# Halved weight places and a seven-block second expert layer in a two-layer diffusion backbone

## The chip, the core and the metric

The program runs on one core of a Trainium2 chip, as one launch. The metric is the device time of that launch in microseconds. The engines that matter here are TensorE (PE in the profile; PEld is its weight load, which overlaps), VectorE (DVE), ScalarE (ACT), GpSimd (POOL) and the sync engine SP, whose queue issues nearly all loads from HBM; ACT's queue issues a few.

## The reference, cut to what matters

Two layers act on 256 latent tokens and 256 context tokens of width 1024. Each layer has a mixer (layer 0: grouped attention beside a Fourier mix; layer 1: differential attention), then a mixture of 16 experts, each a gated MLP of inner width 512. A token takes one group of four experts and, in it, the best two:

```python
g_idx = jnp.argmax(g_logits, axis=-1)
e_sel = jnp.take_along_axis(e_logits, g_idx[:, None, None], axis=1)[:, 0]
top_p, top_i = lax.top_k(jax.nn.softmax(e_sel, axis=-1), TOP_K)
...
def expert_step(acc, params):
    wg, wu, wd, gate = params
    y = (jax.nn.silu(tok @ wg) * (tok @ wu)) @ wd
    return acc + gate[:, None] * y, None
```

Layer 0 runs its experts on 512 tokens (1024 choices), layer 1 on the 256 latent tokens (512 choices). All weights are float32: an expert has three matrices of 2 MB (gate, up, down), so a layer's experts are 96 MB.

## The kernel before

**Slots and blocks.** The experts of a layer are ranked by how many tokens chose them (four of layer 1, two of layer 0 are fixed experts that keep the last ranks, so that their weights can be fetched before the ranking is known). `CAPS` gives each rank a number of slots, `PLAN` packs the slots into blocks of 128 rows. Kind "m" is one expert of 128 slots, "p" two of 64, "q" four of 32, and "w" is made of the two largest: one block of 128 slots for each and one block that holds the ends of both, 64 + 64. Layer 1 has eight blocks: block 0 (ranks 12 to 15), 1 (rank 3), 2 (rank 2), 3 (the ends of ranks 0 and 1), 4 (rank 0), 5 (rank 1), 6 (ranks 8 to 11), 7 (ranks 4 to 7). Should an expert have more tokens than slots, a general path behind a branch computes the rest. With these inputs the counts of layer 1 are 141, 127, 70 and 56 for ranks 0 to 3 and at most 27 behind them, so the branch is not taken before, nor with the slots of the changed kernel.

**Products.** Each block goes through three products: G (gate), U (up) and D (down). G and U are eight steps over the 128-row slices of the weights (`gate_up`), D is four slices for two halves of the output (`down`), again eight steps. In one step every expert of the block has a matmul of its own: its 128, 64 or 32 slots are the columns of the array that it uses, and 512 columns of its weights stream through. So a step has one matmul (128 wide), two (64 wide each, side by side) or four (32 wide). Ahead of a block's G stand 48 small matmuls that pick its tokens (`pick`), between U and D four transposes (`tr`), and behind D eight matmuls that scatter the result to the tokens (`sp`). In layer 1 the order of the 24 products is written out by hand in `TURNS`; the order of single instructions on an engine inside that is set when the program is built.

**Weights.** `piece` gives out places of 16 KB for each of the 128 partitions, 2 MB: a ring of four (`RING`), and further ones in rooms that are free at that time (`more["first"]`, `more["order"]`; in layer 1 nine places in all, 18 MB). One place holds one matrix of an expert, and one DMA fills it (`load`). A place comes free when the last matmul on it is done. `Experts.todo` lists the loads in the order of the products, and `issue` puts the next ones on SP's queue. In layer 0 the last three loads, the up matrix of rank 7 and the down matrices of ranks 6 and 7, stand on ACT's queue behind the output writes (`yd`) of the last block but one, since their places come free late. The same places carry the modulation weights (`wada`) and the projections (`win`, `wi`, `wo`).

Of the kernel before, what the change touches and what calls it, by code (L numbers as in the profile page):

```python
# [19 lines left out]
P = 128  # L20
D = 1024
KT = 8
# [11 lines left out]
    (192, 192) + (128,) * 2 + (32,) * 12,  # L34
)

# [3 lines left out]
    (("q", 12, 13, 14, 15), ("m", 3), ("m", 2), ("w", 0, 1), ("q", 8, 9, 10, 11), ("q", 4, 5, 6, 7)),  # L40
# [28 lines left out]
TURNS = ("G0 U0 G1 U1 D0 D1 G6 G4 U6 U4 G3 G5 D6 U3 D4 U5 D3 D5 G7 G2 U2 U7 D2 D7")  # L69
# [96 lines left out]
def hybrid_kernel(ctx: ExitStack, tc: tile.TileContext, A: dict, dbg=None):  # L166
# [4 lines left out]
    RING = 4  # L171
# [159 lines left out]
    def ada_load(l, pair, q, after=None):  # L331
        w = piece([P, 2, 2048], "wada")
        src = A["w_ada"][l].rearrange("(p k) n -> p k n", p=P)
        load(w, src[:, 2 * q:2 * q + 2, 2048 * pair:2048 * pair + 2048], after)
        ada_w[l, pair, q] = w

    def ada_mm(l, pair, q):
        if q == 0:
            ada_ps[l, pair] = aux("ada")
        ps = ada_ps[l, pair]  # L340
        w = ada_w.pop((l, pair, q))
        for k in range(2):
            kt = 2 * q + k
            for j in range(4):
                T.matmul(ps[32 * j:32 * j + 32], cs[:, kt, :], w[:, k, 512 * j:512 * j + 512],  # L345
                         start=(kt == 0), stop=(kt == KT - 1))
# [29 lines left out]
    def ada_first_load(s):  # L376

        w = piece([P, KT, 2, 256], "wada0")
        src = A["w_ada"][0].rearrange("(p k) (g n) -> p k g n", p=P, g=6)
        nc.sync.dma_start(w, src[:, :, 0:2, 256 * s:256 * s + 256])  # L380
        ada_w["first", s] = w
# [12 lines left out]
    def ada_first(s):  # L394
        w = ada_w.pop(("first", s))
        ps = aux("ada")
        for kt in range(KT):
            for j in range(4):
                T.matmul(ps[32 * j:32 * j + 32, 0:128], cs[:, kt, :], w[:, kt, j // 2, 128 * (j % 2):128 * (j % 2) + 128],
                         start=(kt == 0), stop=(kt == KT - 1))  # L400
# [34 lines left out]
    def load_cols(name, src, c0, n=512, after=None):  # L435
        w = piece([P, KT, n], name)
        load(w, src.rearrange("(k p) n -> p k n", p=P)[:, :, c0:c0 + n], after)
        return w

    def project(wk, hT, groups, tick, order=None, start=None, early=None):  # L440
# [10 lines left out]
        for i in range(-n, len(flat) + AHEAD):  # L451
# [4 lines left out]
            if i < 0 or n <= i < len(flat):  # L456
# [6 lines left out]
                split(*parts[j], w()[:, kt, :])  # L463
# [18 lines left out]
    def out_project(wk, yT, w, g1, tbs, hook, done, place):  # L482


        for h in range(2):
            sp = [[wk.tile([P, 512], F32R, name="wo", bufs=KT), place[:, kt, :]] for kt in range(KT)]
            for n, tb in enumerate(tbs):
                ps = mm()
                for kt in range(KT):
                    if n == 0:  # L490
                        split(*sp[kt], w[h][:, kt, :])
# [12 lines left out]
    def layer_even(fill):  # L504
# [7 lines left out]
        w_a = piece([P, KT, 512], "win")  # L512
        for s in range(4):
# [6 lines left out]
            nc.sync.dma_start(w_a[:, 2 * s:2 * s + 2, :], src[:, 2 * s:2 * s + 2, 512:1024])  # L520
# [468 lines left out]
    class Experts:  # L989


        def __init__(self, l):
# [3 lines left out]
            self.todo = list(dict.fromkeys((r, which) for which, b in products(l) for _, _, r in blocks[b]))  # L996
# [3 lines left out]
        def issue(self, n=None, after=None, queue=None):  # L1000
            n = len(self.todo) if n is None else n
            for r, which in self.todo[:n]:
                self.load(r, which, after, queue)
            del self.todo[:n]

        def load(self, r, which, after, queue):
# [8 lines left out]
            w, src = weights(pick, which, lambda s, n: piece(s, n, True))  # L1015
            load(w, src, after, queue)
            self.w[r, which] = w
# [11 lines left out]
    def weights(pick, which, place):  # L1029
        w = place([P, KT, 512] if which < 2 else [P, 4, D], "we")  # L1030
        return w, pick(A[("w_gate", "w_up", "w_down")[which]]).rearrange("(p k) n -> p k n", p=P)

    def moe(l, ntb, experts, yp, yT, finish, w_o, place, after_loads):
# [8 lines left out]
        if l == 0:  # L1042
            hp = more["H"] = left("h2")
            rows_of = hp.tile([P, ntb, D], F32, name="h2", tag="piece", bufs=1)
        h2 = [xt[:, 2 + tb, :] if l else rows_of[:, tb, :] for tb in tbs]


        if l:
            fp = more["F"] = left("first")
            experts.issue(1)  # L1050
# [131 lines left out]
        experts.issue(2 - l)  # L1182
# [156 lines left out]
        experts.issue(len(fixed) - 2 + l)  # L1339
# [135 lines left out]
        if l == 0:  # L1475
# [10 lines left out]
            experts.issue(1)  # L1486
            experts.issue(len(experts.todo) - 7)
            g2 = piece([P, nv + 2, D], "g2", True)
# [17 lines left out]
        experts.issue(len(experts.todo) - (0 if l else 3))  # L1506
# [117 lines left out]
        def weights_at(i, k):  # L1624
            which, b = ops[i]
            w = experts.w[blocks[b][0][2], which]
            return w[:, k, :] if which < 2 else w[:, k // 2, 512 * (k % 2):512 * (k % 2) + 512]
# [8 lines left out]
        def gate_up(which, bi, amid):  # L1636

            ps = mm("gu")
            for kt in range(KT):
# [7 lines left out]
                for _, n_, r in blocks[bi]:  # L1647
                    T.matmul(ps[c:c + n_], xTs[bi][0][:, kt, c:c + n_], experts.w[r, which][:, kt, :],  # L1648
# [13 lines left out]
        def down(bi, amid, final):  # L1662
# [7 lines left out]
            for f in range(4):  # L1670
# [3 lines left out]
                for h in range(2):  # L1674
# [5 lines left out]
                    for _, n_, r in blocks[bi]:  # L1680
                        T.matmul(ps[h][c:c + n_], aTs[bi][0][:, f, c:c + n_],  # L1681
                                 experts.w[r, 2][:, f, 512 * h:512 * h + 512], start=(f == 0), stop=(f == 3))
# [9 lines left out]
            else:  # L1692
# [8 lines left out]
                if bi == len(blocks) - 2:  # L1701
                    for _ in range(3):
# [3 lines left out]
        for i, (which, bi) in enumerate(ops):  # L1706
# [22 lines left out]
            if final and which == 0:  # L1729
# [3 lines left out]
                after_loads(gather(0, [g2[:, nv + k, :] for k in range(2)]))  # L1733
# [8 lines left out]
        with tc.If(rv > 0):  # L1742
            if l == 0:
                more["first"] = 2 * ["E"] + ["H"]
            spare = lambda s, n: piece(s, n, True)
# [14 lines left out]
            with tc.For_i(0, NE, 1) as e:  # L1760
# [3 lines left out]
                with tc.If(nc.values_load(some[0:1, 0:1], min_val=0, max_val=1) > 0):  # L1764
                    ws = []
                    for i in range(3):
                        w, src = weights(pick, i, spare)
                        G.dma_start(w, src)
                        ws.append(w)
                    rc = un.tile([P, ntb], F32, name="rc")  # L1770
                    G.dma_start(rc, restd[bass.ds(e, 1)].rearrange("o p t -> (o p) t"))
                    for tb in range(ntb):
# [16 lines left out]
                        for which in range(2):  # L1789
                            ps = tr("gu")  # L1790
                            for kt in range(KT):
                                T.matmul(ps, xT_[:, kt, :], ws[which][:, kt, :], start=(kt == 0), stop=(kt == KT - 1))
# [9 lines left out]
                        for h in range(2):  # L1802
                            ps = tr("dn")
                            for f in range(4):
                                T.matmul(ps, aT[:, f, :], ws[2][:, f, 512 * h:512 * h + 512], start=(f == 0), stop=(f == 3))
# [73 lines left out]
    def second_parts(n):  # L1879

        return more["X"].tile([P, KT, 512], F32R, name="lo", tag="piece", bufs=n)

    yp, yT = layer_even(fill0)
    more["first"] = 4 * [None] + ["X"] + 2 * ["E"]
    place = second_parts(1)
    more["order"] = [None, "H"] + 3 * [None] + ["X"] + 2 * ["E"]
    ex = Experts(0)
    ex.issue(4)
# [18 lines left out]
    def first_experts():  # L1907
        more["first"], more["order"] = [], 2 * [None] + 2 * ["X"] + 2 * [None] + ["F", "X", "E"]
        w_odd["place"] = second_parts(3)
        ex = Experts(1)  # L1910
        ex.issue(6)
# [39 lines left out]
```

## Time and profile before

| | before |
|---|---|
| runs | 1064.57, 1067.69, 1064.04 us; median 1064.57 us |
| the profiled execution | 1060.02 us, its span 1058.3 us |
| TensorE busy | 977.3 us, 92% of the span |
| VectorE, ScalarE, GpSimd busy | 53%, 38%, 5% |
| moved by DMA | 309.81 MB, 293 GB/s over the span |
| second expert layer, first product to last | 814.96 to 1043.2 us |

The profiled execution lies 4.55 us below the median of the runs. In the profile a 512-column float32 matmul leaves two records, and four 32-wide matmuls that run side by side leave eight, so counts of instructions ("x64") are records. A row of the timeline joins neighbours of one line and sometimes of several widths; the width named is that of the first.

### The profile page before, as it was taken

The page shows a single profiled execution, that of the slowest core. Times are in us where ns is not written, and L with a number is a line of the kernel's source. Part 1 is how long each engine was busy: PE and PEld are TensorE (multiplying, and loading weights), DVE is VectorE, ACT ScalarE, POOL GpSimd, SP SyncE. Part 2 cuts the span into 40 slices and gives each one's busy share as a digit, 9 for nine tenths or more (in the row PEclk, how much of TensorE's full clock was granted, in tenths as well). Part 3 has the DMA queues.
Part 4 walks back from the last instruction along what each step waited for, and adds up shares of the span by engine and source line. Part 5 has one row for each costly group of instructions (what it writes and reads, how often), then busy time and mean ns, then how long its engine had stood idle before and what let it go on. Part 6 is the DMA issues. An engine that isn't in the chain of part 4 may idle for free. (4 is left out here: it accounts for less than half of the span.)

```text
span 1058.3 us, 14182 instructions
## 1 busy us (share of the span) xinstructions
PE 977.3 (92%) x5205; PEld 573.3 (54%) x5205; DVE 556.4 (53%) x1354; ACT 397.3 (38%) x817; POOL 48.9 (5%) x73
## 2 busy tenths in 40 slices
PE   3899999897999899999978999998788999999995
PEld 3676555686455454666423578875565444434531
DVE  3565465877456543677327557438787223214324
ACT  4255343643235233666205435327764211100111
POOL 3000100100100000000021000000000000000000
PEclk9999999999999999999988999999998999999998
DMA  9969877535779998999897674433155999969891
GB/s 287 367 272 384 341 324 280 212 128 217 299 289 429 387 430 354 358 357 351 314 367 275 232 256 159 145 121 133 50 210 195 399 427 427 427 272 426 360 408 41
DMA packets 52546, 309.81 MB, mean 293 GB/s; under 512 B 4432, under 2 KB 12832, under 8 KB 35064
## 3 DMA queue, kind: packets, MB, share of 16 engines
q1 hardware_dynamic: 42440, 277.01, 66.0%
q0 software_dynamic: 5984, 19.26, 5.1%
q10 hardware_dynamic: 4048, 12.59, 3.2%
q8 instruction: 43, 0.70, 0.3%
q14 instruction: 31, 0.25, 0.1%
HBM read 299.85 MB, written 8.98 MB: 292 GB/s over the span
## 5 line engine op out<-in xcount | busy, mean ns | idle before, releaser
L1648 PE MATMUL gu<-we,xT 128*64 128x512 f32 (+1 forms) x512 | 116.7, 616 | 4.3 <-DMA we<-in_w_up_dram 4.3
L1681 PE MATMUL dn<-we,aT 128*64 128x512 f32 (+2 forms) x480 | 117.3, 597 | 0.1
L312 ACT CAST wh<-we 128x512 fp32r<-128x512 f32 x144 | 85.4, 621 | 53.6 <-PE dn L317 27.4
L1648 PE MATMUL gu<-we,xt 128*32 128x512 f32 (+2 forms) x448 | 104.8, 596 | 0.0
L316 PE MATMUL mm<-wh,hT 128*128 128x512 f32 x248 | 101.1, 407 | 1.8 <-ACT hT L312 1.8
L317 PE MATMUL mm<-wh,hT 128*128 128x512 f32 x248 | 98.2, 396 | 0.7 <-DVE hT L313 0.7
L313 DVE TENSOR_TENSOR wl<-we,wh 128x512 fp32r<-128x512 f32 x144 | 92.5, 688 | 11.7 <-ACT wh L312 8.4
L318 PE MATMUL mm<-wl,hT 128*128 128x512 f32 x248 | 98.0, 395 | 0.0
L1681 PEld LDWEIGHTS dn<-we,aT 128*64 128x64 f32 (+2 forms) x480 | 36.3, 132 | 64.1 <-issue 61.4
L1648 PEld LDWEIGHTS gu<-we,xt 128*32 128x32 f32 (+2 forms) x448 | 36.6, 136 | 57.8 <-issue 56.1
L1648 PEld LDWEIGHTS gu<-we,xT 128*64 128x64 f32 (+1 forms) x512 | 33.4, 134 | 63.1 <-issue 56.8
L1659 DVE TENSOR_TENSOR sg<-sg,gu 128x256 f32<-128x256 f32 x40 | 15.2, 418 | 97.1 <-PE gu L1648 94.6
L313 DVE TENSOR_TENSOR wl<-wi,wh 128x512 fp32r<-128x512 f32 x52 | 35.7, 689 | 48.5 <-ACT wh L312 33.4
L316 PEld LDWEIGHTS mm<-wh,hT 128*128 128x128 f32 x248 | 47.2, 190 | 18.2 <-issue 6.7
L312 ACT CAST wh<-wi 128x512 fp32r<-128x512 f32 x52 | 32.1, 622 | 66.3 <-PE mm L317 61.9
L317 PEld LDWEIGHTS mm<-wh,hT 128*128 128x128 f32 x248 | 47.1, 190 | 11.6 <-issue 1.7
L318 PEld LDWEIGHTS mm<-wl,hT 128*128 128x128 f32 x248 | 47.0, 190 | 11.4 <-issue 0.8
L312 ACT CAST y<-y 128x512 fp32r<-128x512 f32 x16 | 9.9, 618 | 94.1 <-DVE y L1579 81.2
L1654 ACT ACTIVATE sg<-gu 128x512 f32<-128x512 f32 x20 | 11.9, 597 | 88.0 <-PE gu L1648 82.6
L345 PE MATMUL ada<-wada,cs 128*32 128x512 f32 x320 | 39.7, 599 | 3.0 <-DMA wada<-in_w_ada_dram 3.0
L316 PE MATMUL mm<-wo,yT 128*128 128x512 f32 x96 | 40.1, 418 | 2.4 <-ACT wo L312 2.4
L1389 DVE TENSOR_SCALAR oh<-cst,slots 128x128 bf16<-128x128 f32 (+1 forms) x96 | 23.4, 278 | 33.0 <-PE tok L1265 32.0
(367 smaller groups left out, 1665.1 us busy)
## 6 DMA issues: line engine op xcount, KB each, us to landing
we<-in_w_gate_dram SPq DMA_DIRECT2D x32, 2048.0 KB, 15.3
we<-in_w_up_dram SPq DMA_DIRECT2D x31, 2048.0 KB, 13.2
we<-in_w_down_dram SPq DMA_DIRECT2D x30, 2048.0 KB, 19.1
wada<-in_w_ada_dram SPq DMA_DIRECT2D x24, 2048.0 KB, 10.5
wi<-in_w_in_odd_dram SPq DMA_DIRECT2D x6, 2048.0 KB, 7.9
win<-in_w_in_even_dram SPq DMA_DIRECT2D x2, 2048.0 KB
wo<-in_w_out_even_dram SPq DMA_DIRECT2D x2, 2048.0 KB, 8.4
we<-in_w_down_dram ACTq DMA_DIRECT2D x2, 2048.0 KB
```

What stands on the lines that cost most here:

```text
L312: S.copy(hi, src)
L313: V.tensor_tensor(out=lo, in0=src, in1=hi.bitcast(F32), op=ALU.subtract)
L316: T.matmul(ps, a[0], b[0], start=start, stop=False)
L317: T.matmul(ps, a[1], b[0], start=False, stop=False)
L318: T.matmul(ps, a[0], b[1], start=False, stop=stop)
L345: T.matmul(ps[32 * j:32 * j + 32], cs[:, kt, :], w[:, k, 512 * j:512 * j + 512], start=(kt == 0), stop=(kt == KT - 1))
L1389: V.tensor_scalar(o[:, c:c + n_], C("iota128")[:, 0:n_], float(s0), slot[k][:, tb:tb + 1], op0=ALU.add, op1=ALU.is_equal)
L1648: T.matmul(ps[c:c + n_], xTs[bi][0][:, kt, c:c + n_], experts.w[r, which][:, kt, :], start=(kt == 0), stop=(kt == KT - 1))
L1654: S.activation(parted(sgs[bi], 4), by_part(ps, 4), AF.Silu)
L1659: V.tensor_tensor(out=sg[:, c], in0=sg[:, c], in1=up[:, c], op=ALU.mult)
L1681: T.matmul(ps[h][c:c + n_], aTs[bi][0][:, f, c:c + n_], experts.w[r, 2][:, f, 512 * h:512 * h + 512], start=(f == 0), stop=(f == 3))
```

## The change

Two things change. **The places.** Every place of 2 MB becomes two of 1 MB (`RING` 4 to 8, the lists of rooms doubled), and each load becomes two DMAs of 1 MB, each into its own place: slices 0 to 3 and 4 to 7 of a gate or up matrix, slices 0, 1 and 2, 3 of a down matrix. `part` finds the slice. A block's first halves are issued ahead of all its second halves. `issue` counts halves; ACT's queue takes the last six halves instead of the last three loads. The rows of the second norm of layer 0 and of `g2` get two places instead of one.

**The plan of layer 1.** The two largest get 160 slots instead of 192 and rank 3 gets 64 instead of 128. The new kind "x" makes the block of ends from 32 + 32 slots of ranks 0 and 1 and the 64 of rank 3; rank 3's own block goes. Seven blocks and 21 products are left: block 0 (ranks 12 to 15), 1 (rank 2), 2 (rank 0), 3 (rank 1), 4 (the ends and rank 3), 5 (ranks 8 to 11), 6 (ranks 4 to 7).

```diff
-    (192, 192) + (128,) * 2 + (32,) * 12,
+    (160, 160) + (128, 64) + (32,) * 12,
...
-    (("q", 12, 13, 14, 15), ("m", 3), ("m", 2), ("w", 0, 1), ("q", 8, 9, 10, 11), ("q", 4, 5, 6, 7)),
+    (("q", 12, 13, 14, 15), ("m", 2), ("x", 0, 1, 3), ("q", 8, 9, 10, 11), ("q", 4, 5, 6, 7)),
...
-        if kind == "w":
-            pair = [(base[r] + 128, 64, r) for r in rs]
-            ones = [[(base[r], 128, r)] for r in rs]
-            blocks += [pair] + ones if layer else [ones[0], pair, ones[1]]
+        if kind in "wx":
+            ends = [(base[r] + 128, CAPS[layer][r] - 128, r) for r in rs[:2]]
+            ones = [[(base[r], 128, r)] for r in rs[:2]]
+            blocks += ones + [ends + [(base[rs[2]], 64, rs[2])]] if kind == "x" else [ones[0], ends, ones[1]]
...
-TURNS = ("G0 U0 G1 U1 D0 D1 G6 G4 U6 U4 G3 G5 D6 U3 D4 U5 D3 D5 G7 G2 U2 U7 D2 D7")
+TURNS = ("G0 U0 D0 G2 U2 G4 U4 D2 G3 U3 D4 D3 G6 U6 G1 G5 U1 D6 U5 D1 D5")
...
-    RING = 4
+    RING = 8
...
+    def part(w, k):
+
+        n = w[0].shape[1]
+        return w[k // n][:, k % n, :]
...
-            self.todo = list(dict.fromkeys((r, which) for which, b in products(l) for _, _, r in blocks[b]))
+            self.todo = list(dict.fromkeys((r, which, h) for which, b in products(l) for h in range(2)
+                                           for _, _, r in blocks[b]))
...
-    def weights(pick, which, place):
-        w = place([P, KT, 512] if which < 2 else [P, 4, D], "we")
-        return w, pick(A[("w_gate", "w_up", "w_down")[which]]).rearrange("(p k) n -> p k n", p=P)
+    def weights(pick, which, h):
+
+        w = piece([P, 4, 512] if which < 2 else [P, 2, D], "we", True)
+        n = w.shape[1]
+        return w, pick(A[("w_gate", "w_up", "w_down")[which]]).rearrange("(p k) n -> p k n", p=P)[:, n * h:n * h + n, :]
...
-        experts.issue(len(experts.todo) - (0 if l else 3))
+        experts.issue(len(experts.todo) - (0 if l else 6))
...
-                    T.matmul(ps[c:c + n_], xTs[bi][0][:, kt, c:c + n_], experts.w[r, which][:, kt, :],
+                    T.matmul(ps[c:c + n_], xTs[bi][0][:, kt, c:c + n_], part(experts.w[r, which], kt),
...
-                    for _ in range(3):
+                    for _ in range(6):
                         experts.issue(1, queue=S)
...
-        more["first"], more["order"] = [], 2 * [None] + 2 * ["X"] + 2 * [None] + ["F", "X", "E"]
+        more["first"], more["order"] = [], 4 * [None] + 4 * ["X"] + 4 * [None] + 2 * ["F"] + 2 * ["X"] + 2 * ["E"]
```

How the instructions stand now, first on TensorE in layer 1. In the kernel before, the up product of the block of ends (64 + 64, `xt` are its tokens) and that of rank 1 stand like this, behind the picks of another block, with `tr` the transposes and `dn` the down product of a block of four experts:

```order
L1648 MATMUL gu<-we,xt 64x512 x4
L1609 MATMUL tr<-cst,sg 128x128 x4
L1648 MATMUL gu<-we,xt 64x512 x8
L1648 MATMUL gu<-we,xt 128x512 x8
L1681 MATMUL dn<-we,aT 32x512 x6
L1648 MATMUL gu<-we,xt 64x512
L1681 MATMUL dn<-we,aT 32x512 x26
```

In the changed kernel the gate product of the block of ends stands behind a scatter (`sp`); the first half of it:

```order
L1597 MATMUL sp<-y_7900,hot 128x512
L1659 MATMUL gu<-we,xt 32x512 x2
L1659 MATMUL gu<-we,xt 64x512
L1659 MATMUL gu<-we,xt 32x512 x2
L1659 MATMUL gu<-we,xt 64x512
L1659 MATMUL gu<-we,xt 32x512 x2
L1659 MATMUL gu<-we,xt 64x512
L1659 MATMUL gu<-we,xt 32x512 x2
L1659 MATMUL gu<-we,xt 64x512
L1620 MATMUL tr<-cst,sg 128x128 x4
```

What moved: a run of matmuls of one width has become an alternation of 32, 32 and 64 wide, once in each of the eight steps, and the up and the down product of this block alternate in the same way.

The other place is ACT's queue near the end of layer 0. Before, behind the writes of the last block but one:

```order
L1699 DMA yd<-y 64x512 x3
L211 ISA
L211 DMA we<-in_w_up_dram 128x4096
L211 ISA
L211 DMA we<-in_w_down_dram 128x4096
L211 ISA
L211 DMA we<-in_w_down_dram 128x4096
L1518 COPY swt<-tr 128x512
```

In the changed kernel, at the same place:

```order
L1710 DMA yd<-y 64x512 x3
L217 ISA
L217 DMA we<-in_w_up_dram 128x2048
L217 ISA
L217 DMA we<-in_w_up_dram 128x2048
L217 ISA
L217 DMA we<-in_w_down_dram 128x2048
L217 ISA
L217 DMA we<-in_w_down_dram 128x2048
```

What moved: the two up DMAs here are the second halves of ranks 6 and 7; the first half of rank 7's up matrix now stands on SP's queue, so it no longer waits behind these writes.

## Rows read from the trace of the kernel before

**Rows 1.** The page: busy time, share of the span and instructions of each engine.

```profile
PE 977.3 (92%) x5205; PEld 573.3 (54%) x5205; DVE 556.4 (53%) x1354; ACT 397.3 (38%) x817; POOL 48.9 (5%) x73
```

**Rows 2.** Layer 1's experts in stretches of 20 us.

```profile
core 0: us, PE busy (x) PEld busy (x) DVE busy (x) ACT busy (x) POOL busy (x), PEclk, DMA share, GB/s
...
840.00:860.00 20.00, 19.10 (x133) 9.36 (x133) 3.08 (x12) 2.04 (x4) 0.00 (x0) 1.00 1.01 429
...
940.00:960.00 20.00, 19.36 (x75) 7.95 (x71) 7.63 (x13) 1.29 (x3) 0.00 (x0) 1.00 0.54 218
```

**Rows 3.** Timeline of TensorE, a block's parts (start, length, engine, line, tiles, records).

```profile
814.96 7.07 PE L1648 MATMUL gu<-we,xT 128*32 128x512 f32 x64
...
837.19 0.60 PE L1609 MATMUL tr<-cst,sg 128*128 128x128 f32 x4
837.62 10.46 PE L1648 MATMUL gu<-we,xt 128*128 128x512 f32 x24
...
985.89 2.43 PE L1586 MATMUL sp<-y,hot 128*128 128x512 f32 x8
988.25 1.92 PE L1648 MATMUL gu<-we,xt 128*32 128x512 f32 x16
990.10 2.85 PE L1316 MATMUL pick<-pick,h 128*128 128x128 bf16 x48
...
993.08 5.36 PE L1648 MATMUL gu<-we,xt 128*32 128x512 f32 x48
```

**Rows 4.** The same timeline where the width changes.

```profile
932.76 1.92 PE L1681 MATMUL dn<-we,aT 128*32 128x512 f32 x12
934.61 1.07 PE L1648 MATMUL gu<-we,xt 128*64 128x512 f32 x2
935.61 7.05 PE L1681 MATMUL dn<-we,aT 128*32 128x512 f32 x52
```

**Rows 5.** Timeline of TensorE's weight loads (PEld) at those places.

```profile
933.65 0.12 PEld L1681 LDWEIGHTS dn<-we,aT 128*32 128x32 f32 x3 [0.31 <-issue]
934.61 0.19 PEld L1648 LDWEIGHTS gu<-we,xt 128*64 128x64 f32 x2 [0.84 <-issue]
```

**Rows 6.** Timeline of SP's queue in layer 1: issues of weights.

```profile
907.96 18.16 SPq L211 DMA_DIRECT2D we<-in_w_down_dram  x2
950.00 4.82 SPq L211 DMA_DIRECT2D we<-in_w_gate_dram  x5
...
999.02 15.57 SPq L211 DMA_DIRECT2D we<-in_w_down_dram  x5
```

**Rows 7.** Timeline of TensorE, the last product and the scatter behind it.

```profile
1036.13 7.07 PE L1681 MATMUL dn<-we,aT 128*32 128x512 f32 x56
1043.89 0.50 PE L1586 MATMUL sp<-y,hot 128*128 128x512 f32 x1 [0.69 <-ACT y L312]
```

**Rows 8.** Timeline of TensorE at the end of layer 0.

```profile
537.46 9.96 PE L1648 MATMUL gu<-we,xT 128*64 128x512 f32 x30 [4.34 <-DMA we<-in_w_up_dram]
...
548.95 7.95 PE L1681 MATMUL dn<-we,aT 128*64 128x512 f32 x32
556.83 3.70 PE L1553 MATMUL ylast<-y,swt 128*128 128x512 f32 x8
```

**Rows 9.** Stretches at the end of layer 0, and two while modulation weights are loaded.

```profile
536.40:543.30 6.90, 5.84 (x14) 1.71 (x16) 0.00 (x0) 0.00 (x0) 2.35 (x3) 0.51 1.02 435
543.30:550.00 6.70, 5.99 (x26) 1.89 (x24) 1.57 (x4) 1.15 (x1) 0.00 (x0) 1.00 0.98 407
...
575.00:580.00 5.00, 4.74 (x17) 2.63 (x17) 4.14 (x8) 3.19 (x6) 0.00 (x0) 1.00 1.00 423
600.00:605.00 5.00, 3.06 (x22) 1.31 (x14) 1.39 (x2) 0.65 (x2) 0.00 (x0) 1.00 0.99 415
```

**Rows 10.** What SP's queue waited for over the whole run (total, times, longest).

```profile
SPq L211 <- PE gu L1648: 156.2, 18, 23.0
...
SPq L211 <- DMA yd<-y: 93.9, 9, 23.5
```

More of the change, by code (lines that the diff above doesn't have):

```diff
@@ L331, in ada_load @@
     def ada_load(l, pair, q, after=None):
-        w = piece([P, 2, 2048], "wada")
         src = A["w_ada"][l].rearrange("(p k) n -> p k n", p=P)
-        load(w, src[:, 2 * q:2 * q + 2, 2048 * pair:2048 * pair + 2048], after)
-        ada_w[l, pair, q] = w
+        ada_w[l, pair, q] = [piece([P, 1, 2048], "wada") for k in range(2)]
+        for k, w in enumerate(ada_w[l, pair, q]):
+            load(w, src[:, 2 * q + k:2 * q + k + 1, 2048 * pair:2048 * pair + 2048], after)
     def ada_mm(l, pair, q):
@@ L376, in ada_first_load @@
     def ada_first_load(s):
-        w = piece([P, KT, 2, 256], "wada0")
         src = A["w_ada"][0].rearrange("(p k) (g n) -> p k g n", p=P, g=6)
-        nc.sync.dma_start(w, src[:, :, 0:2, 256 * s:256 * s + 256])
-        ada_w["first", s] = w
+        ada_w["first", s] = [piece([P, KT, 256], "wada0") for g in range(2)]
+        for g, w in enumerate(ada_w["first", s]):
+            nc.sync.dma_start(w, src[:, :, g, 256 * s:256 * s + 256])
     b0 = {}
@@ L435, in load_cols @@
     def load_cols(name, src, c0, n=512, after=None):
-        w = piece([P, KT, n], name)
-        load(w, src.rearrange("(k p) n -> p k n", p=P)[:, :, c0:c0 + n], after)
-        return w
+        ws = [piece([P, 4, n], name) for h in range(2)]
+        for h, w in enumerate(ws):
+            load(w, src.rearrange("(k p) n -> p k n", p=P)[:, 4 * h:4 * h + 4, c0:c0 + n], after)
+        return ws
     def project(wk, hT, groups, tick, order=None, start=None, early=None):
@@ L462, in project @@
                     parts[j] = [wk.tile([P, 512], F32R, name=r, bufs=AHEAD + 1) for r in ("wh", "wl")]
-                split(*parts[j], w()[:, kt, :])
+                split(*parts[j], part(w(), kt))
             if i >= AHEAD:
@@ L485, in out_project @@
         for h in range(2):
-            sp = [[wk.tile([P, 512], F32R, name="wo", bufs=KT), place[:, kt, :]] for kt in range(KT)]
+            sp = [[wk.tile([P, 512], F32R, name="wo", bufs=KT), part(place, kt)] for kt in range(KT)]
             for n, tb in enumerate(tbs):
@@ L490, in out_project @@
                     if n == 0:
-                        split(*sp[kt], w[h][:, kt, :])
+                        split(*sp[kt], part(w[h], kt))
                     c = slice(128 * tb, 128 * tb + 128)
@@ L511, in layer_even @@
         wk = right("proj")
-        w_a = piece([P, KT, 512], "win")
+        w_a = [piece([P, 4, 512], "win") for h in range(2)]
         for s in range(4):
@@ L1001, in issue, with load @@
             n = len(self.todo) if n is None else n
-            for r, which in self.todo[:n]:
-                self.load(r, which, after, queue)
+            for r, which, h in self.todo[:n]:
+                self.load(r, which, h, after, queue)
             del self.todo[:n]
-        def load(self, r, which, after, queue):
+        def load(self, r, which, h, after, queue):
             if r >= self.known:
@@ L1043, in moe @@
             hp = more["H"] = left("h2")
-            rows_of = hp.tile([P, ntb, D], F32, name="h2", tag="piece", bufs=1)
-        h2 = [xt[:, 2 + tb, :] if l else rows_of[:, tb, :] for tb in tbs]
+            rows_of = [hp.tile([P, 2, D], F32, name="h2", tag="piece", bufs=2) for v in range(2)]
+        h2 = [xt[:, 2 + tb, :] if l else part(rows_of, tb) for tb in tbs]
         if l:
             fp = more["F"] = left("first")
-            experts.issue(1)
+            experts.issue(2)
         wk = right("out")
@@ L1181, in moe @@
         fixed = list(itertools.takewhile(lambda p: p[0] >= experts.known, experts.todo))
-        experts.issue(2 - l)
+        experts.issue(4 - 2 * l)
         def tl(shape, name, dt=F32):
@@ L1338, in moe @@
         picks = {i: pick_first(i) for i in range(1, len(fixed_of)) if l == 0}
-        experts.issue(len(fixed) - 2 + l)
+        experts.issue(len(fixed) - 4 + 2 * l)
         key = tl([NE], "key")
@@ L1626, in weights_at @@
             w = experts.w[blocks[b][0][2], which]
-            return w[:, k, :] if which < 2 else w[:, k // 2, 512 * (k % 2):512 * (k % 2) + 512]
+            return part(w, k) if which < 2 else part(w, k // 2)[:, 512 * (k % 2):512 * (k % 2) + 512]
         def split_to(i, k):
@@ L1681, in down @@
                         T.matmul(ps[h][c:c + n_], aTs[bi][0][:, f, c:c + n_],
-                                 experts.w[r, 2][:, f, 512 * h:512 * h + 512], start=(f == 0), stop=(f == 3))
+                                 part(experts.w[r, 2], f)[:, 512 * h:512 * h + 512], start=(f == 0), stop=(f == 3))
                         c += n_
@@ L1732, in moe @@
                     pass
-                after_loads(gather(0, [g2[:, nv + k, :] for k in range(2)]))
+                after_loads(gather(0, [rooms0[:, k, :] for k in range(2)]))
             if final and which == 2:
@@ L1743, in moe @@
             if l == 0:
-                more["first"] = 2 * ["E"] + ["H"]
-            spare = lambda s, n: piece(s, n, True)
+                more["first"] = 4 * ["E"] + 2 * ["H"]
             over = un.tile([P, ntb, NE], F32, name="over", tag="sg", bufs=SG)
@@ L1766, in moe @@
                     for i in range(3):
-                        w, src = weights(pick, i, spare)
-                        G.dma_start(w, src)
-                        ws.append(w)
+                        ws.append([])
+                        for h in range(2):
+                            w, src = weights(pick, i, h)
+                            G.dma_start(w, src)
+                            ws[i].append(w)
                     rc = un.tile([P, ntb], F32, name="rc")
@@ L1791, in moe @@
                             for kt in range(KT):
-                                T.matmul(ps, xT_[:, kt, :], ws[which][:, kt, :], start=(kt == 0), stop=(kt == KT - 1))
+                                T.matmul(ps, xT_[:, kt, :], part(ws[which], kt), start=(kt == 0), stop=(kt == KT - 1))
                             gu.append(ps)
@@ L1804, in moe @@
                             for f in range(4):
-                                T.matmul(ps, aT[:, f, :], ws[2][:, f, 512 * h:512 * h + 512], start=(f == 0), stop=(f == 3))
+                                T.matmul(ps, aT[:, f, :], part(ws[2], f)[:, 512 * h:512 * h + 512], start=(f == 0), stop=(f == 3))
                             t = un.tile([P, DE], F32, name="sg", bufs=SG)
@@ L1879, in second_parts @@
     def second_parts(n):
-        return more["X"].tile([P, KT, 512], F32R, name="lo", tag="piece", bufs=n)
+        return [more["X"].tile([P, 4, 512], F32R, name="lo", tag="piece", bufs=n) for h in range(2)]
     yp, yT = layer_even(fill0)
-    more["first"] = 4 * [None] + ["X"] + 2 * ["E"]
-    place = second_parts(1)
-    more["order"] = [None, "H"] + 3 * [None] + ["X"] + 2 * ["E"]
+    more["first"] = 8 * [None] + 2 * ["X"] + 4 * ["E"]
+    place = second_parts(2)
+    more["order"] = 2 * [None] + 2 * ["H"] + 6 * [None] + 2 * ["X"] + 4 * ["E"]
     ex = Experts(0)
-    ex.issue(4)
+    ex.issue(8)
     def load_odd(i, after=None):
```

21 lines of the change are left out of this document (11 added, 10 removed).

## The prediction, made before the change was run

> **What bounds the kernel now.** I read the busy times first: TensorE works 92% of the span, VectorE just over half [rows 1]. So a block of layer 1 that disappears is worth what it costs on TensorE, unless weights come too late. The stretches of layer 1 show both limits at once: TensorE at 19.1 of 20 us and the DMA engines full at 429 GB/s from 840 on, and then, at 940 to 960, the DMA engines only 0.54 busy while TensorE goes on [rows 2]. The reader is to see there that transfers are ahead and have run out of places: SP's queue issues nothing between the two down loads ending at 926 and the gate loads from 950 [rows 6]. Last I read the two ends: the last product starts at 1036.13 without a wait, and 1058.3 - 1043.2 = 15 us of scatter, norm and output behind it don't change [rows 7]; in layer 0 there is one wait for weights, 4.34 us [rows 8].
>
> **The block removed.** A product of eight steps takes about 6.9 us from its start to the next one's, whatever its split: four 32-wide matmuls in a step share the array and leave together, as the first gate product shows (64 records in 7.07 us, which is 16 passes of 0.43 us with four records each), and so twelve 128-wide ones in a row take 10.46 us (24 records), again a step in 0.86 [rows 3]. A block has three products, 3 x 6.9 = 20.7; its picks, 2.98 (990.10 to 993.08); its scatter, 2.36 (985.89 to 988.25); its transposes, 0.44 (837.19 to 837.62) [rows 3]. Together 26.5 us. All of it lies on TensorE, so it is on the path.
>
> **The block that is now mixed.** In each step the block of ends has 32, 32 and 64 columns. Whether these run side by side decides the case, and no row shows a step of two widths. The nearest rows are those where the width changes between products: six 32-wide matmuls, two steps, take 1.85 us to the next start; then one 64-wide matmul, between 32-wide ones, takes 1.00 us to the next start, where a step without a change of width takes 0.86 [rows 4]. And its weights are loaded only at 934.61, the moment at which it starts, with PEld idle for 0.84 us ahead of that, while loads of an unchanged width come 0.31 us after the last one, beside the running matmul [rows 5]. So a change of width is a full stop: what runs ends, then weights are loaded, then the next starts. These rows are of widths that share columns; the changed kernel's don't share any. I take it that the stop holds there too, since the late weight load needs no other explanation than the width. Then a step costs 0.98 (the two 32-wide ones, between 1.85 / 2 and 1.00) + 1.00 (the 64-wide one) = 1.98 instead of 0.86, 1.12 more, times 8 steps and 3 products = 26.9 us. The other bound is 0, all three side by side. I take 26.9, and keep 0 as a rival.
>
> [...]
>
> The two terms cancel: -26.5 + 26.9 = +0.4 us on TensorE. Three products of 6.9 + 9.0 = 15.9 us hold the places of three experts.
>
> **The end of layer 1.** What TensorE doesn't decide, the places do. Up to the first gate product of block 5 (ranks 8 to 11) the changed order has 9 plain products (62.1), 3 mixed (47.7), 4 picks (11.9), 3 scatters (7.1), 4 transposes (1.8) and some 2 us for steps that are cut in two by other work: 132.6, so it starts near 814.96 + 132.6 = 947.6. Behind it stand 9 products that need 6 x 8 + 3 x 2 = 54 halves of weights: twice as dense as what came ahead, because blocks 5 and 6 now stand together at the end. The 18 places can hold at most 16 of these (two are still under the down product of rank 1), so 38 are to be fetched from then on. At 427 GB/s (just under the rates of [rows 2]) a half of 1.0486 MB takes 2.456 us: 93.3 us, to 1040.9; and behind the last half come four steps, 3.5 us: 1044.4. TensorE alone would need 9 x 6.9 + 2 picks (6.0) + 3 scatters (7.1) + transposes and cut steps (5) = 80 us, to 1028. So transfers set the end there, at 1044.4 where the last product before ended at 1043.2 [rows 7]: +1.2. To that comes what a half costs more than half of a whole. Modulation weights are loaded now in rows of 8 KB, which is what the gate and up halves keep at best; they moved at 423 and 415 GB/s [rows 9] against 429, 1.4 to 3.3% of 93 us, 1 to 3 us. And each issue waits for its place, twice as often as now: 0 to 3 us where the queue runs dry. I take +4 for the end of layer 1, bounds +1 and +8. It can't be much below, since the places hold no more; a start of block 5 some us earlier would move it by as much.
>
> **The end of layer 0.** [...] I take 0, bounds -3 and +4. Everything of layer 1 stands behind it, so it counts in full. The projections and the modulation weights in halves I cost at nothing: their waits are on first pieces, and TensorE finds other work; bounds -1 and +1.
>
> **Sum.** The profiled span changes by +0.4 + 4 + 0 = +4.4: 1060.0 to 1064.4. The median of before stands 4.55 us above its profiled execution, so I forecast 1064.57 + 4.4 = 1069.
>
> **Rivals.** (a) **The widths run side by side.** Then the 26.9 us fall away and only the block removed counts. For it speaks that the four 32-wide matmuls do just that [rows 3], and that 32, 32 and 64 share no column; against it the late weight load [rows 5]. The end of layer 1 holds a part back: block 5 starts 27 us earlier, near 921, and the same 97 us of transfers behind it end at 1018, 25 us before now, if the places are full by then; DMA idles less in shorter products, so I take 6 of it off: 19 us, 1046, between 1038 and 1053. [...]
>
> (b) **Transfers pay in both layers** (the other side). Rank 7's late half holds up layer 0 (+4), and the end of layer 1 pays the upper bound (+7), since the long mixed products let the DMA engines idle and block 5 and 6 then wait for halves: 1064.57 + 0.4 + 4 + 7 = 1076, between 1071 and 1080. It decides once block 5 starts later than 950 or a half takes above 2.5 us. For it speak the places that are full already before [rows 6], against it that a half comes free earlier than a whole.
>
> (c) **Halves repay in layer 0.** The wait of 4.34 and the slow clock go, -3, and the end of layer 1 costs 1: 1064.57 + 0.4 - 3 + 1 = 1063, between 1058 and 1065. For it speaks that the first half of the up matrix no longer stands behind ACT's writes.
>
> That the change does not do what it says, by more tokens than slots, the counts exclude.
>
> **How the numbers follow.** The forecast (1064 to 1071) gets 0.36, (a) 0.21, (b) 0.30, (c) 0.13. A measurement of this kernel tells about 0.5%, 5.3 us, from no change: 1059.2 to 1069.9 is the same. Faster: (a) and a sixth of (c), 0.23. Slower: (b) and a third of the forecast, 0.42. Same: the rest, 0.35. The range must reach into (a) to leave no more than 2 in 10 out: 1047 to 1077. Without (a) it would be 1059 to 1077.
>
> **What would show it.** In the profile after, the gate rows of the mixed block: a 64-wide row of 1.0 us between 32-wide ones of 1.0 us, and some 16 us for the product, show the stop; 7 us for it show (a). Block 5's start near 948, a DMA share of 1.0 from there to the end, and waits of the last up and down product on weights show the term at the end; a share well under 1 there, with TensorE waiting, shows that issues and not transfers are late. A wait at the end of layer 0 longer than 4.3 us shows (b), none shows (c). The forecast is wrong if mixed steps take less than 1.5 us, or if the last down product of layer 1 ends before 1040.

## The result, and the profile after

The changed kernel is slower: 1074.68 us (median of 7 runs, 1071.18 to 1078.03) beside 1065.66 us of the kernel before (7 runs), a ratio of 1.0089 with the 95% interval 1.0066 to 1.0112. Run again later beside the experiments it gave 1.0072 (1.0044 to 1.0100). The profiled execution took 1074.14 us, its span 1071.5 us. Names below: block 6 holds ranks 4 to 7, block 5 ranks 8 to 11, block 4 is the mixed one. The tail is what layer 1 does from G6 on. The prediction called the first block of the tail "block 5"; by the turns it is block 6 (G6); the sums are the same, since both are blocks of four.

The weight loads of the first mixed product (PEld, start, length, tiles, records, idle time ahead), in the changed kernel:

```profile
868.97 0.14 PEld L1659 LDWEIGHTS gu<-we,xt 128*32 128x32 f32 x4 [0.36 <-DVE sg L1670]
869.95 0.19 PEld L1659 LDWEIGHTS gu<-we,xt 128*64 128x64 f32 x2 [0.84 <-issue]
870.95 0.14 PEld L1659 LDWEIGHTS gu<-we,xt 128*32 128x32 f32 x4 [0.81 <-issue]
871.93 0.19 PEld L1659 LDWEIGHTS gu<-we,xt 128*64 128x64 f32 x2 [0.84 <-issue]
872.94 0.14 PEld L1659 LDWEIGHTS gu<-we,xt 128*32 128x32 f32 x4 [0.81 <-issue]
```

These rows answer [rows 5]. Now the widths alternate inside a product and share no column, and the same 0.84 and 0.81 us of idle time stand before each load. From one 32-wide pair to the next it is 870.95 - 868.97 = 1.98 us: 0.98 for the pair, 1.00 for the 64-wide matmul. The product on the timeline of TensorE (a row joins both widths under the first), with four transposes in its middle:

```profile
868.97 8.01 PE L1659 MATMUL gu<-we,xt 128*32 128x512 f32 x24
876.91 0.66 PE L1620 MATMUL tr<-cst,sg 128*128 128x128 f32 x4
877.49 8.99 PE L1659 MATMUL gu<-we,xt 128*32 128x512 f32 x28
```

Four steps take 8 us (24 records, six to a step), and the whole product stands from 868.97 to about 885.4: 15.9 us without the transposes, where a step of one width took 0.86 [rows 3].

Layer 1 in stretches, the columns as in [rows 2]:

```profile
900.00:920.00 20.00, 20.00 (x55) 8.19 (x54) 5.06 (x10) 1.83 (x3) 0.00 (x0) 1.00 0.34 116
...
940.00:960.00 20.00, 20.00 (x131) 9.33 (x134) 9.56 (x19) 3.92 (x7) 0.00 (x0) 1.00 0.62 234
960.00:980.00 20.00, 20.00 (x204) 10.01 (x198) 4.21 (x12) 3.00 (x6) 0.00 (x0) 1.00 0.99 397
980.00:1000.00 20.00, 20.00 (x106) 7.45 (x97) 1.51 (x4) 1.78 (x3) 0.00 (x0) 1.00 1.01 418
1000.00:1020.00 20.00, 17.85 (x109) 6.46 (x111) 6.87 (x12) 2.52 (x3) 0.00 (x0) 1.00 1.01 421
1020.00:1040.00 20.00, 15.59 (x65) 5.09 (x54) 1.53 (x5) 0.29 (x1) 0.00 (x0) 0.91 1.01 420
```

Between 900 and 920, at the end of the second mixed product and behind it, the DMA engines are busy only 0.34: SP's queue waits for TensorE there (from 890 to 960 it waits 39.3 us, in six waits, for gate and up matmuls), so the places are full of weights that the slow products still need. From 960 on the DMA engines are full, and it is TensorE that falls to 15.6 of 20 us. The tail begins with G6 in the first row here and ends with the last row (TensorE):

```profile
955.86 7.07 PE L1659 MATMUL gu<-we,xt 128*32 128x512 f32 x64
...
1018.11 3.63 PE L1659 MATMUL gu<-we,xt 128*32 128x512 f32 x28 [0.28 <-DMA we<-in_w_up_dram]
1023.11 1.05 PE L1659 MATMUL gu<-we,xt 128*32 128x512 f32 x2 [1.37 <-DMA we<-in_w_up_dram]
1025.75 1.04 PE L1659 MATMUL gu<-we,xt 128*32 128x512 f32 x2 [1.59 <-DMA we<-in_w_up_dram]
1028.24 5.06 PE L1659 MATMUL gu<-we,xt 128*32 128x512 f32 x26 [1.45 <-DMA we<-in_w_up_dram]
...
1053.14 3.62 PE L1692 MATMUL dn<-we,aT 128*32 128x512 f32 x20 [0.59 <-DMA we<-in_w_down_dram]
```

Before, the last down product ran without a wait [rows 7]; now the last up product of a block of four (all but its first matmul, which ran earlier) is cut by four waits and takes from 1016.78 to 1033.2, 16.4 us. The first gate product of layer 1 began at 822.69 and the last down product ended at 1056.76: 234.07 us, where it was 228.24 before. So layer 1 costs 5.8 us more.

### The profile page after: what moved, and what is told of

Read it like the earlier page. It is cut to its first block, busy times and chain, and to the rows that moved or that the text cites. A ratio compares the mean times of both kernels' runs of the same rounds, so it can differ in the third digit from the quotient of the medians.

```text
span 1071.5 us, 14441 instructions
## 1 busy us (share of the span) xinstructions
PE 990.6 (92%) x5139; PEld 565.0 (53%) x5139; DVE 548.4 (51%) x1334; ACT 394.1 (37%) x811; POOL 49.9 (5%) x73
## 5 line engine op out<-in xcount | busy, mean ns | idle before, releaser
L1692 PE MATMUL dn<-we,aT 128*32 128x512 f32 (+2 forms) x480 | 123.5, 612 | 5.3 <-DMA we<-in_w_down_dram 5.0
L1659 PE MATMUL gu<-we,xt 128*32 128x512 f32 (+2 forms) x448 | 112.1, 612 | 4.7 <-DMA we<-in_w_up_dram 4.7
L1692 PEld LDWEIGHTS dn<-we,aT 128*32 128x32 f32 (+2 forms) x480 | 34.8, 131 | 75.2 <-issue 61.2
L1659 PEld LDWEIGHTS gu<-we,xt 128*32 128x32 f32 (+2 forms) x448 | 32.1, 130 | 72.5 <-issue 61.7
L324 PE MATMUL mm<-lo,yT 128*128 128x512 f32 x96 | 38.8, 406 | 1.1 <-DVE lo L319 1.1
L322 PE MATMUL gu<-wh,xT 128*128 128x512 f32 x96 | 39.1, 407 | 0.8 <-ACT wh L318 0.8
## 6 DMA issues: line engine op xcount, KB each, us to landing
we<-in_w_down_dram SPq DMA_DIRECT2D x60, 1024.0 KB, 10.1
```

The costliest lines, as they stand in the source:

```text
L322: T.matmul(ps, a[0], b[0], start=start, stop=False)
L324: T.matmul(ps, a[0], b[1], start=False, stop=stop)
L1659: T.matmul(ps[c:c + n_], xTs[bi][0][:, kt, c:c + n_], part(experts.w[r, which], kt), start=(kt == 0), stop=(kt == KT - 1))
L1692: T.matmul(ps[h][c:c + n_], aTs[bi][0][:, f, c:c + n_], part(experts.w[r, 2], f)[:, 512 * h:512 * h + 512], start=(f == 0), stop=(f == 3))
```

## The experiments

All ratios are to the kernel before, run on the same chip. Beside each stands what the trace shows of layer 1, from the first gate product to the end of the last down product, since the time ahead of it moves from one execution to the next by more than the effects looked for there: the plan-only kernel, in which only layer 1's plan and turns differ from before, began them at 822.7, 7.8 us later than the profiled execution of before. That one was early: it took 1060.02 us, and the 17 runs of the kernel before beside these experiments have a median of 1064.91. Each kernel but the changed one was profiled once; the two profiles of the changed kernel agree in layer 1 within 0.1 us.

**The plan alone, with whole places.** Edits: `CAPS`, `PLAN`, `block_plan` and `TURNS` as in the change, everything else as before.

> The kernel before with the new plan of layer 1 alone (slots, blocks, turns); places and loads stay whole, 2 MB. Theory (a change of width stops the array; transfers set the end of layer 1): the mixed products last 16 to 17 us as in the changed kernel, nothing changes ahead of layer 1's experts, and the end of layer 1 comes about 4.5 us later than before (8 whole places hold 16 MB ahead, 19 loads of 4.9 us follow, then a whole product of 6.9 us): +4 us, ratio 1.004 (1.001 to 1.008). Rival H (halving costs, the plan is neutral): 1.000. Rival P (the plan costs all of it): 1.009.

Measured: 1080.99 us, ratio 1.0153 (1.0114 to 1.0193); layer 1 took 245.3 us. No theory had that: the plan alone costs 16 us, more than the whole change. Its tail, from G6 on, shows what whole matrices cost there:

```profile
960.27 7.07 PE L1649 MATMUL gu<-we,xt 128*32 128x512 f32 x64
...
1016.48 5.77 PE L1682 MATMUL dn<-we,aT 128*32 128x512 f32 x49 [2.99 <-DMA we<-in_w_down_dram]
...
1036.08 8.54 PE L1649 MATMUL gu<-we,xt 128*32 128x512 f32 x58 [3.84 <-DMA we<-in_w_up_dram]
...
1060.96 7.05 PE L1682 MATMUL dn<-we,aT 128*32 128x512 f32 x52 [1.11 <-DMA we<-in_w_down_dram]
```

The tail lasts 1068.0 - 960.3 = 107.7 us, where it is 100.9 in the changed kernel: a place of 2 MB comes free later, so that more is left to move (393 GB/s over this tail are 42.3 MB, 397 GB/s over that of the changed kernel 40.1 MB), and the product waits for all of a matrix. The other 4.4 us lie ahead of G6 (137.5 us from the first gate product, 133.2 in the changed kernel). Most of them are the first down product, which whole places leave cut in three by other work, as it was before:

```profile
839.99 1.91 PE L1682 MATMUL dn<-we,aT 128*32 128x512 f32 x8 [0.18 <-DVE aT L1616]
...
844.81 1.90 PE L1682 MATMUL dn<-we,aT 128*32 128x512 f32 x4
...
849.62 7.05 PE L1682 MATMUL dn<-we,aT 128*32 128x512 f32 x52
```

Its pieces add up to 10.7 us; the halved kernel has two pieces of 16 and 48 records, 7.3 us. In the first rows here two or one matmul run in a pass instead of four (8 and 4 records in 1.9 us, where four abreast leave 16).

**The halves alone, with the old plan.** Edits: the change with the four pieces above as before.

> The changed kernel with the old plan of layer 1 (eight blocks, no block of two widths); places and loads stay halved. Theory: the profile of the changed kernel was already 7.7 us late at the first gate product of layer 1, with 5 us of it from the last two products of layer 0; that stays, and layer 1 itself costs what it did before (228 us from the first gate product to the last down product, perhaps 2 less since a half comes free earlier): +5 us, ratio 1.005 (1.002 to 1.008). Rival H (halving costs all of it): 1.009. Rival P (only the plan costs): 1.000.

Measured: 1064.97 us, ratio 0.9994 (0.9973 to 1.0014): nothing. Layer 1 took 224.8 us, 3.4 less than before. The first down product still stands in three pieces here, but these take 9.0 us where they took 10.7; the rest of the 3.4 was not traced. The theory had put 7.7 us ahead of layer 1 down to the change, and most of that was the early execution of before. What is left is small. Timed difference less the difference in layer 1 gives what halves cost ahead of layer 1's experts: here -0.6 + 3.4 = 2.8; with the new plan (the changed kernel, mean of its two medians, against the plan alone) -7.8 + 11.2 = 3.4; with the two kernels of 32-wide groups below -10.4 + 11.6 = 1.2. So 1 to 3.5 us, near the limit of what these runs tell. The profiles show where they lie: in layer 0's experts. From their first product to the first one behind them (`ylast` in [rows 8]) the three kernels with whole places (before, the plan alone, and the one with 32-wide groups below) take 287.7, 289.4 and 288.4 us, and the seven profiles with halves 291.1 to 295.2, in the mean 4.5 more. From `ylast` to layer 1's first gate product halves take 1.8 less in the mean; there the two groups overlap.

**One width for all: rank 3 as two groups of 32.** The 64 slots of rank 3 are multiplied in two matmuls of 32 columns with the same weights, four per step:

```diff
+        def columns(bi):
+            n = min(n_ for _, n_, _ in blocks[bi])
+            return [(n, r) for _, n_, r in blocks[bi] for _ in range(n_ // n)]
...
-                for _, n_, r in blocks[bi]:
+                for n_, r in columns(bi):
```

(the same in `down`).

> The changed kernel, where the 64 slots of rank 3 are multiplied as two groups of 32 columns with the same weights, so that every matmul of the mixed block is 32 wide (four per step instead of three). Theory (a change of width stops the array): the mixed products fall from 16 to 17 us to 6.9 us each, 27 to 29 us less on TensorE up to block 5; the 97 to 101 us of transfers from there on stay, so layer 1 ends about 20 to 25 us earlier: 1052 us, ratio 0.987 (0.980 to 0.993). Rival (it is not the width but three experts in one block, or their weights' arrival, that makes these products long): they stay above 13 us, ratio 1.006 to 1.012.

Measured: 1045.72 us, ratio 0.9814 (0.9779 to 0.9849): 26 to 29 us faster than the changed kernel and 19 faster than the one before, for the same slots, the same turns and one matmul more in each step. The first mixed product on the timeline of TensorE, then the first product of the tail:

```profile
870.09 3.64 PE L1663 MATMUL gu<-we,xt 128*32 128x512 f32 x32
873.66 0.66 PE L1620 MATMUL tr<-cst,sg 128*128 128x128 f32 x4
874.24 4.49 PE L1663 MATMUL gu<-we,xt 128*32 128x512 f32 x36
...
931.59 7.07 PE L1663 MATMUL gu<-we,xt 128*32 128x512 f32 x64
```

Four steps in 3.57 us where they took 8; G6 begins 107.6 us after the first gate product where it was 133.2: 25.6 us less. And the tail lasts 1032.5 - 931.6 = 100.9 us, as in the changed kernel: TensorE came 25.6 us earlier, and the tail did not change. As much is left to move in it (399 GB/s over it are 40.2 MB), and the DMA engines of this kernel have no room before it either: they are full from 840 to 1020.

```profile
840.00:860.00 20.00, 19.50 (x155) 9.94 (x156) 6.53 (x22) 3.28 (x6) 0.00 (x0) 1.00 1.01 418
940.00:960.00 20.00, 20.00 (x181) 9.81 (x176) 4.32 (x14) 2.99 (x6) 0.00 (x0) 1.00 1.01 420
1000.00:1020.00 20.00, 17.12 (x58) 5.63 (x58) 4.63 (x9) 1.53 (x3) 0.00 (x0) 0.91 1.02 422
```

The prediction's rival (a), no cost for mixed widths, had a price of 1046 us; this kernel without mixed widths takes 1045.72.

**The same groups with whole places.**

> The kernel before with the new plan and the 64 slots of rank 3 as two groups of 32 columns; places and loads whole. Theory: nothing of the 7.7 us ahead of layer 1's experts, mixed products of 6.9 us, layer 1 ends some 20 us earlier than before: 1046 us, ratio 0.982 (0.975 to 0.989), the fastest of the four. Rival (halves are what lets the seven blocks pay, since whole places wait longer for transfers at the end): no faster than the halved one with the same groups, 0.987 or more.

Measured: 1056.14 us, ratio 0.9910 (0.9876 to 0.9944). The theory had this as the fastest; it is 10 us slower than with halves, and the rival holds. Layer 1 took 220.1 us, 112.0 up to G6 and 108.1 in the tail: against the halved kernel 4.4 and 7.2 more, close to the 4.4 and 6.8 of the plan-only kernel. So halves are worth 11 us in layer 1 with seven blocks, 3.4 with eight. With seven blocks the two effects add up: the mixed widths cost 25.2 us with whole places (245.3 - 220.1) and 25.6 with halves (234.1 - 208.5).

**All 32-wide matmuls first, then all 64-wide.** In the changed kernel, a mixed product runs its eight steps for ranks 0 and 1 and then eight for rank 3 (`widths` holds the wide ones back until the last step).

> The changed kernel, where the mixed block's products do all eight steps of their two 32-wide matmuls first and then all eight of the 64-wide one: the same matmuls, two changes of width in a product instead of sixteen. It divides the cost of a mixed step (2.00 us measured, 0.86 for a step of one width) into work that isn't side by side (0.86) and the stops themselves (0.28). Theory: the products take 2 x 6.9 = 13.7 to 14.0 us where they took 16 to 17, 6 to 9 us less up to the tail, and transfers at the end hold some of it back: 2 to 8 us under the changed kernel, ratio to before 1.001 to 1.007. Rival (only the alternation costs, tiles of two widths do run side by side in longer runs): products near 7 us, ratio 0.98 to 0.99.

Measured: 1069.65 us, ratio 1.0044 (1.0022 to 1.0066); layer 1 took 230.7 us. The weight loads of the first product where the width changes:

```profile
873.36 0.12 PEld L1673 LDWEIGHTS gu<-we,xt 128*32 128x32 f32 x2 [0.31 <-issue]
873.79 0.12 PEld L1673 LDWEIGHTS gu<-we,xt 128*32 128x32 f32 x2 [0.31 <-issue]
874.74 0.19 PEld L1673 LDWEIGHTS gu<-we,xt 128*64 128x64 f32 x2 [0.84 <-issue]
875.22 0.14 PEld L1673 LDWEIGHTS gu<-we,xt 128*64 128x64 f32 x1 [0.29 <-issue]
```

Inside a width the loads run 0.31 or 0.29 us after the one before; at the one change 0.84. The 64 columns of rank 3 are free all the time, and still their loads wait for the last 32-wide matmul. The product takes 867.04 to 881.75, 14.1 us without its transposes: so of the 9 us that a mixed product costs over one of one width, 7 are work that isn't side by side and about 2 the stops themselves. Of three products' 5.4 us the end of layer 1 came 3.4 earlier.

**The tail with fewer bytes.** In the changed kernel, ranks 8 to 11 fetch one slice of each half, and all steps use it; the DMAs and matmuls stay, and the kernel leaves out the true result of these four experts.

```diff
+            if self.l == 1 and 8 <= r < 12:
+                load(w[:, 0:1, :], src[:, 0:1, :], after, queue)
```

> The changed kernel, where the weights of ranks 8 to 11 in layer 1 are fetched only in part (one slice of each half, used for all its steps; so the result of these four experts is not computed): the 24 DMAs stay, 16 halves' worth of bytes in them, about 40 us of transfers, is left out. All matmuls stay, mixed products included. Theory (transfers set the end of layer 1): the tail behind the mixed products falls from 100.9 us to what TensorE needs, 80 to 87; 13 to 20 us under the changed kernel, ratio to before 0.990 to 0.997. Rival (TensorE or something else sets the end): no faster than the changed kernel by more than 4 us, ratio 1.005 to 1.010.

Measured: 1057.06 us, ratio 0.9923 (0.9891 to 0.9954). The tail, 954.61 to 1038.86, lasts 84.25 us instead of 100.90, and TensorE is busy for all of it: what TensorE needs. What it waited for there, in the changed kernel and then with fewer bytes (total, times, longest):

```profile
PE gu L1659 <- DMA we<-in_w_up_dram: 4.7, 4, 1.6
PE sp L1597 <- ACT y L318: 3.3, 4, 1.0
PE dn L1692 <- DMA we<-in_w_down_dram: 0.9, 2, 0.6
```

```profile
PE sp L1605 <- ACT y L322: 1.5, 2, 0.9
PE sp L1605 <- DVE y L323: 0.4, 1, 0.4
```

The reader is to see that the waits named, 4.7 + 0.9, are a third of the 16.65 us that left the tail. Where one of four experts' halves lands late, three matmuls of a step have run and the fourth runs alone (the two rows x2 in the tail of the changed kernel, 1.05 and 1.04 us); that counts as busy.

**Another order of the turns.** The block of ranks 4 to 7 stands between the mixed products, so that its loads fall where the DMA engines had room.

> The changed kernel with another order of layer 1's products: the gate, up and down products of ranks 4 to 7 stand between the mixed ones (G0 U0 D0 G2 U2 G6 G4 U6 U4 D2 G3 U3 D6 D4 D3 G1 G5 U1 U5 D1 D5), where the DMA engines had room (0.34 and 0.62 busy), instead of in the tail. Mixed products stay as they are. Theory (the dense tail is what transfers pay): 24 halves move out of the tail, and layer 1 ends 5 to 12 us earlier than in the changed kernel: ratio to before 0.998 to 1.004. Rival (the places, not the order, set the transfers): within 3 us of the changed kernel, 1.006 to 1.012.

Measured: 1067.50 us, ratio 1.0021 (0.9997 to 1.0046); layer 1 took 228.8 us, 5.3 less than in the changed kernel, at the lower end of the theory, and as much as before (228.2). The order matters, and here it wins back what layer 1 had lost and no more. The changed kernel beside these runs:

> The changed kernel once more, as the partner of these runs on the same chip: 1.009 of before (1.0066 to 1.0112 so far).

Measured: 1071.62 us, ratio 1.0072 (1.0044 to 1.0100); layer 1 took 234.1 us once more, with G6 133.2 us after the first gate product, though it began at 818.5, 4 us earlier than in the first profile.

## Why the prediction was right, point by point

**The mixed step** was forecast at 1.98 us and measured at 1.98; the product at 15.9 and measured at 15.9 (G4). The reading of [rows 4, 5], that the late weight load belongs to the change of width and not to shared columns, holds: the loads of the 64-wide tiles wait in columns that nobody else uses, with 0.84 us of idle time before each, and with one width for all 25.6 us go. Rival (a) falls. Tiles of one width run side by side (four 32-wide matmuls in 0.86 us [rows 3]); the 32-wide pair and the 64-wide matmul of a step ran one behind the other here, 0.98 and 1.00 us.

**The two terms cancel**: G6 was forecast 132.6 us after the first gate product and came after 133.2. The sum counts what is left of them, +0.4, twice: the end of layer 1 was worked out from 947.6, which already holds both terms. So it should have read +4.0 and not +4.4.

**The end of layer 1**: from G6 on 93.3 us of transfers and 3.5 of steps were forecast, 96.8, with 1 to 6 us for halves that move more slowly and for issues; measured 100.9. From there on 38 halves were to be fetched, and 38.2 halves' worth moved (40.1 MB). It shows as the transfers' time and not TensorE's in two ways: fewer bytes give 84.25 us, and an earlier TensorE gives 100.9 again. The halves of the changed kernel ran at 418 to 421 GB/s where the DMA engines were full, whole matrices at 426 to 429 in the plan-only kernel, 1.8% apart: 1.7 us of these 4. Of layer 1 in all, +4.4 was forecast and +5.8 came.

**The end of layer 0** was taken as 0 between -3 and +4, and the rest of layer 0's experts had no term at all. The 0 and its bounds, and with them the -3 of (c) and the +4 of (b), were the author's estimates, and no run shows them as terms; in their place the runs say +1 to +3.5 for everything ahead of layer 1's experts. In the means of the profiles it is 2.0 us in layer 0's experts ahead of the four transposes (`tr<-cst,wide`) that stand in its last gate product, 2.5 from there to `ylast`, and 1.8 back behind that. With halves only the last four steps of the last down product must follow the last half, so that it could end earlier. The rows of the changed kernel show it waiting up to those very steps:

```profile
551.07 1.07 PE L1692 MATMUL dn<-we,aT 128*64 128x512 f32 x2
553.41 3.65 PE L1692 MATMUL dn<-we,aT 128*64 128x512 f32 x14 [1.27 <-DMA we<-in_w_down_dram]
557.27 1.04 PE L1692 MATMUL dn<-we,aT 128*64 128x512 f32 x2 [0.22 <-DMA we<-in_w_down_dram]
560.95 6.62 PE L1692 MATMUL dn<-we,aT 128*64 128x512 f32 x14 [2.63 <-DMA we<-in_w_down_dram]
567.50 3.70 PE L1564 MATMUL ylast<-y,swt 128*128 128x512 f32 x8
```

Behind the wait of 2.63 us the granted clock is 0.54 in the mean (560.95 to 567.50) and 0.50 from 561 to 566, and the last 14 records take 6.62 us where 14 records take 3.65 at a granted clock of 1.00 (553.41 to 557.06). From the transposes ahead of it to `ylast` the last down product takes 12.9 to 17.4 us with halves, 8.8 to 10.2 with whole places; the up product before it ends 13.6 to 19.2 us behind the transposes in the gate product with halves, 17.7 to 19.8 with whole places, in the mean 3.0 earlier. So the wait and the slow clock moved from the up product (clock 0.51 in [rows 9], 1.00 from 545.88 to 549.53 in the changed kernel) into the down product: (c), that halves repay there, is right of the up product and falls for the sum.

The waits themselves (0.44, 1.85, 1.27, 0.22 and 2.63 us for the last up and down products, 6.4 in all) are as long as in the plan-only kernel with whole places (5.99 and 0.61); none is above the 4.3 us that the prediction had named as the sign of (b). And the first up half of rank 7, the late half of (b), does wait for output writes: SP's queue stands 10.3 us for them ahead of the second gate halves, and the first up halves of ranks 6 and 7 go out at 525.1 and 527.0, where before the whole up matrix of rank 6 went out at 513.0; the up product did not come later by it. How much of the 4.5 us in layer 0's experts is this wait, and how much the lower rate of halves, no run separates.

The sum was too small by these terms: 4.4 forecast, 7 to 9 measured. Of the 5.7 us by which 1069 missed 1074.68, 1.1 come from the median of before, which rose from 1064.57 to 1065.66 with more runs, 1.4 from layer 1, and the other 3.2 from what lies ahead of its experts.

**Rival (b)**, transfers paying in both layers, at 1076 with 0.30, was nearest to the measured time, 1074.68, which lies in its band (1071 to 1080) and outside the forecast's own (1064 to 1071). Its parts were smaller than it had them: 5.8 us in layer 1 where it had 7.4, and 1 to 3.5 ahead of it where it had 4. The terms were the forecast's, the amounts nearer to those of (b). The chance of slower, 0.42, was the largest of the three.

**Where the reasoning was short.** The value of halves in layer 1 was not in the sum: I had costed the plan against a layer 1 that runs as now, and charged halves with 1 to 6 us. Alone with whole places the plan would have cost 16 us; halves took back 7 to 9 of them. The plan's gain in blocks went to the change of width, its dense tail to transfers, and the halves repaid a part of the tail.

**What it points to.** With the 64 slots as two groups of 32 the seven blocks pay: 1045.72 us, 0.9814 of before, the fastest kernel here. Its DMA engines are full (0.99 to 1.02) from 840 to 1020, so a further gain in layer 1 has to come from bytes or from loads that start earlier, and not from TensorE; this last step is argued, no run of this kernel shows it.

## What to carry to other kernels

Matmuls packed side by side in columns should have one width, as far as 32 beside 64 shows it: a wider expert is better cut into several narrow groups with the same weights than mixed in as it is, since the extra matmul in the step cost nothing here (four steps in 3.57 us) and the mixed widths 25.6 us. A block taken out of TensorE's list pays only if the weights that stand behind it can keep up: count the bytes of the tail against the places that can hold them ahead, before the blocks. And take a stage's cost from start to start, since a late fourth of a step counts as busy time (1.05 and 1.04 us in two rows of the changed kernel).

## What the runs showed of the hardware

A change between 32-wide and 64-wide matmuls stopped TensorE also where the tiles share no column: in the changed kernel 0.81 or 0.84 us without a weight load before each change, 0.98 us for the 32-wide pair and 1.00 for the 64-wide matmul, where a step of one width takes 0.86, and no overlap of the two (1.98 us from one pair to the next). Loads of 1 MB that overlap in the queue (9.7 to 10.1 us from issue to landing in the median, in the changed kernel) ran at 418 to 422 GB/s with rows of 8 KB (the changed kernel and the one with 32-wide groups), against 426 to 429 GB/s for 2 MB with rows of 16 KB (before and the plan alone). Two executions of the changed kernel began layer 1's experts 4.2 us apart (822.7 and 818.5), while layer 1 took 234.1 us in both.
